# w_in multiplied directly in fp32, and GpSimd's tables, splits and taps given to VectorE

## The chip, the cores and the metric

The kernel runs on one core of one Trainium2 chip. The metric is the device time of one execution in microseconds (us). TensorE is PE in the profile, its weight loads are PEld, VectorE is DVE, ScalarE is ACT, GpSimd is POOL, and SyncE, whose queue issues most DMAs, is SP.

## What is computed

One layer of a hybrid backbone for two groups of 128 tokens of width 1024 (a prompt and a sample, so 256 rows in all), everything in fp32:

```
h = rmsnorm(x) * (1 + sc1) + sh1                 # shifts and scales from c @ w_mod
z = h @ w_in + b_in                              # 1024 -> 5120 columns
z_f, z_a, z_b, z_s, z_g = split(z)               # 512, 512, 512, 512, 3 * 1024
br_f = fft2(z_f).real @ w_four
br_c = conformer_conv(z_a * sigmoid(z_b)) @ w_conv_out      # 31 taps, layer norm, silu
y_s  = s5_bidirectional(z_s)                     # 32 groups, 64 complex states, B, C, D
br_s = glu(gelu(y_s)) @ w_ssm_out
x = x + g1 * ((gate_f*br_f + gate_c*br_c + gate_s*br_s) @ w_out)   # gates: sigmoid(z_g)
x = x + g2 * moe(rmsnorm(x) * (1 + sc2) + sh2)   # top 4 of 32 experts, d_ff 1024
```

The weights of all 32 experts are read, 12 MB for each. The outputs are the two normed results and the final S5 states of the prompt.

## The kernel before, in words

The program has two parts. The **front part** is everything up to the routing; the **expert part** then runs the 32 experts one after the other.

The front part is written as some thirty Python generators ("threads") that yield one instruction at a time. While the program is built, class Sched (L55) plays a list scheduler: for each thread's next instruction it works out when its engine and its operands are ready, from a cost that each helper states (mm, tt, stt, act: L264 to L304), adds 0.2 us per unit of the thread's priority (PRIO), and emits the earliest. That fixes the order on each engine; on the chip every engine then runs its list in that order and waits for semaphores. So a cost that is wrong in the plan shows as a wait on the chip. Every operation of a kind has the line of its helper: L273 is every matmul, L262 every transpose, L291 every tensor_tensor, L287 every scalar_tensor_tensor, L304 every activation.

All large weights come through one ring of slots of 1 MB (class Ring, L169): SP issues the loads in one fixed order, each when a slot comes free. The ring begins with slots 0 to 3 and 6 to 9, of which 6 to 9 are dropped after their first use, so four slots serve most of the front part until the S5 result gives it four more.

The parts of the front that matter here:

- modulate (L517) applies the shift and scale to h, eight blocks k of 128 features. For each block it writes h twice: the rounded half hhi (ACT, in the type fp32r) and the rest hlo (DVE, xT - hhi).
- splitter (L1063) and main_products (L1099) do the big products. Each slab of weights (w_in in twenty slabs of 256 columns, then w_four, w_ssm_out and w_conv_out in two each, w_out in four) is cut in four units of 128x512. split (L769) makes the pair: ACT copies a unit to fp32r, and DVE or POOL subtracts that from the original. Who subtracts is chosen by faster (L765), by whose planned clock is behind. Buffers for four units lie in slots 21 and 22. prod3 (L1089) multiplies hi by hi, hi by lo and lo by hi: three fp32r matmuls of 256 columns in place of one in fp32, so 48 matmuls for a slab.
- the order of slabs (seq) is: eight slabs of w_in for z_s, z_f, z_b, z_a, then for each branch (Fourier, S5, conv) and each half of 512 columns two gate slabs of w_in and the slab of the branch's projection, then w_out. Two gate buffers stand between a pair of gate slabs and its projection, so a later pair waits for the projection before it, which waits for its branch (flags mix0, mix2, mix1).
- tables_in (L803) and tables_out (L825) build the S5 matrices: for each of four quarters j, cprod (L783) runs six tensor_tensors of 128x1024 (four products, two sums). Each table has two threads, one on DVE and one on POOL, that take quarters from one list, each with a temporary of its own. m1_transposes (L810) transposes the first table; its quarters 2 and 3 wait for the flag in0, as their slot holds the first slab of w_in.
- taps_sum(j) (L989) sums the 31 taps of the convolution for 128 channels: for j = 0 to 2, 31 scalar_tensor_tensors of 128x256 on DVE; for j = 3 (NP = 1) ACT multiplies and POOL adds. conv (L1007) norms the sum and ends in mix1.
- s5 (L880) runs its scan of 16 steps on DVE, four tensor_tensors of 128x128 each, in a chain; kernel_table (L835) needs all of tables_out and sends its result through DRAM (the tile Kd) back into SBUF, by DMAs on SP's queue.
- fourier (L1037) and the sum over branches (mac, in evacuate, L1157) use slot 20, which held xT before.

The expert part multiplies each expert's 64 gathered rows by 12 slabs in fp32, with scatter products in fp32r. It is not touched by the change.

Of the kernel before, what the change touches and what calls it, by code (L numbers as in the profile page):

```python
# [205 lines left out]
def build(tc, A, O):  # L206
# [3 lines left out]
    with es:  # L210
# [151 lines left out]
        n = 0  # L362
# [73 lines left out]
        start(6, 7, 8, 9)  # L436
# [27 lines left out]
        hhi = new(4, F32R)[:, :].rearrange("p (k t) -> p k t", k=8)  # L464
        hlo = new(5, F32R)[:, :].rearrange("p (k t) -> p k t", k=8)
# [51 lines left out]
        def modulate():  # L517

            for b in range(4):
# [157 lines left out]
        def s5_inputs():  # L677
# [23 lines left out]
            yield tt(tb[2], Bt[:, 1], bch(fr), e="G")  # L701
            yield tt(tb[1], Bt[:, 1], bch(fi))
            yield tt(tb[3], Bt[:, 0], bch(fi), e="G")
            yield tt(Bb[:, 0], tb[0], tb[1], OP.subtract)
            yield tt(Bb[:, 1], tb[2], tb[3], OP.add, e="G")
# [59 lines left out]
        def faster(n, cv, cg):  # L765

            return "V" if sch.t["V"] + n * cv <= sch.t["G"] + n * cg else "G"
# [13 lines left out]
        Mtmp = [tbuf(SL16[:, 1024:2048]), tbuf(SL[11][:, 1024:2048])]  # L781

        def cprod(o_re, o_im, tmp, P, Q, Qi, j, e):  # L783
# [8 lines left out]
            yield tt(o_re, px(0), qx(Q[0]), e=e)  # L792
            yield tt(tmp, px(1), qx(Q[1]), e=e)
            yield tt(o_re, o_re, tmp, OP.subtract, e=e)
            yield tt(o_im, px(0), qx(Q[1] if Qi is None else Qi), e=e)
            yield tt(tmp, px(1), qx(Q[0]), e=e)
            yield tt(o_im, o_im, tmp, OP.add if Qi is None else OP.subtract, e=e)
# [27 lines left out]
        def tables_out(e, tmp, js):  # L825
            yield from need("E", "columns", "pw1")
            while js:
                j = js.pop(0)
                yield from cprod(M2[j][:, :, 0], M2[j][:, :, 1], tmp, pw2, (Ct[:, 0], Ct[:, 1]), nCi, j, e)
# [50 lines left out]
        def s5():  # L880
# [100 lines left out]
            for o in range(4):  # L981
# [3 lines left out]
                yield from split(g2[:, c], m_[:, c], m_[:, 1024 + 256 * o:1280 + 256 * o], e="V")  # L985
# [3 lines left out]
        def taps_sum(j):  # L989
# [17 lines left out]
        def conv():  # L1007
# [23 lines left out]
            for i in range(2):  # L1031
                c = slice(512 * i, 512 * i + 512)
                yield from split(HA[:, c], m_[:, c], m_[:, 1024 + 512 * i:1536 + 512 * i], e="V")
# [3 lines left out]
        def fourier():  # L1037
            yield from need("zf", "columns", "M10", "M11", "M12", "M13")
            UV = SL[20][:, :].rearrange("p (j b c) -> p j b c", j=4, b=2)
# [11 lines left out]
            for i in range(2):  # L1051
                c = slice(512 * i, 512 * i + 512)
                yield from split(PB[6 + i][:, :], m_[:, c], m_[:, 1024 + 512 * i:1536 + 512 * i], e="V")
# [9 lines left out]
        def splitter():  # L1063
# [5 lines left out]
            for key in seq + [("out", q) for q in range(4)]:  # L1069
                for u in UNITS if key == seq[0] else range(4):  # L1070
# [4 lines left out]
                    elif key[0] == "pr":  # L1075
                        src = sl[:, :].rearrange("p (k c) -> p k c", k=4)[:, :, u * 128:(u + 1) * 128]
                    else:
                        src = sl[:, :].rearrange("p (k c) -> p k c", k=8)[:, 4 * (u % 2):4 * (u % 2) + 4,
                                                                          u // 2 * 128:(u // 2 + 1) * 128]
# [5 lines left out]
                    if u == 3:  # L1085
                        ring.done(key)
                        flags.add("in0")
# [11 lines left out]
        def main_products():  # L1099
            nonlocal mh, ml, xa  # L1100
            yield from need("m0")
            for key in seq:
# [8 lines left out]
                for u in UNITS if key == seq[0] else range(4):  # L1111
                    if key[0] == "in":
                        c, first, last = u // 2, u == 0, u % 2 == 1
                        K, xh, xl = range(4 * (u % 2), 4 * (u % 2) + 4), hhi, hlo
                    else:
                        c, first, last = u % 2, u % 2 == 0, True
# [658 lines left out]
```

## Time and profile before

| | before |
|---|---|
| time, median of 3 runs | 1414.85 us (1414.38 to 1416.57) |
| the profiled execution: time; span | 1418.22 us; 1416.4 us |
| PE, PEld busy | 1243.9 us (88%), 655.7 us (46%) |
| DVE, ACT, POOL busy | 492.4 us (35%), 301.5 us (21%), 216.0 us (15%) |
| mean granted clock of PE | 0.961 |
| moved from HBM | 472.6 MB, 335 GB/s over the span |

The shares are means over two unlike parts. In forty slices of 35.4 us the page shows POOL at 4 to 6 tenths in the first ten slices and at 0 in nearly all later ones; DVE is at 7 to 9 tenths in the same ten and at 1 after them; the DMA engines are at 3 to 9 tenths in the first ten and at 8 or 9 in most later ones.

### The profile page before, as it was taken

Reading aid. Unit: us, or ns where it says so; the run is one execution under the profiler, and the core shown is the slowest. Engines: PE = TensorE matmul, PEld = TensorE weight load, DVE = VectorE, ACT = ScalarE, POOL = GpSimd, SP = SyncE. Lnnn points to the kernel's source line nnn. Section 1 sums busy time; section 2 is a strip of 40 time slices with the busy share of each in tenths; the row PEclk is TensorE's granted clock in tenths of the full one; section 3 lists DMA queues with packets and bytes.
Section 4 is the critical chain, followed back from the end, with each engine's and each line's share of the span. In section 5 each row is a group of like instructions: output and inputs, shape, how many; then the busy total and the mean of one; then the engine's idle time right before and its main releaser. Section 6 shows DMA issues by size and latency. Waiting matters only on the chain. (4 is left out here: it accounts for less than half of the span.)

```text
span 1416.4 us, 19588 instructions
## 1 busy us (share of the span) xinstructions
PE 1243.9 (88%) x7444; PEld 655.7 (46%) x7444; DVE 492.4 (35%) x839; ACT 301.5 (21%) x609; POOL 216.0 (15%) x183
## 2 busy tenths in 40 slices
PE   4596787899999999999989999999999989999994
PEld 3475686789833433334343433333334334343331
DVE  7949898897511111111111111111121111211113
ACT  4454344454311101011100101101011101111011
POOL 4555556565300000000000000000000000000001
PEclk9798899999999999999999999999999999999996
DMA  9563489558799999999998999998999994999990
GB/s 268 193 210 115 144 146 266 188 196 316 290 352 410 416 397 415 416 416 415 417 415 319 407 417 414 415 400 357 416 416 416 416 409 185 413 415 415 414 395 33
DMA packets 124834, 477.08 MB, mean 337 GB/s; under 512 B 11871, under 2 KB 49505, under 8 KB 90864
## 3 DMA queue, kind: packets, MB, share of 16 engines
q1 hardware_dynamic: 121744, 468.25, 85.3%
q0 software_dynamic: 2288, 5.76, 1.2%
q8 instruction: 120, 1.97, 0.6%
q10 hardware_dynamic: 624, 0.63, 0.1%
q14 instruction: 58, 0.48, 0.1%
HBM read 472.61 MB, written 1.61 MB: 335 GB/s over the span
## 5 line engine op out<-in xcount | busy, mean ns | idle before, releaser
L273 PE MATMUL pb<-sl,sl 128*64 128x512 f32 (+4 forms) x5344 | 951.3, 485 | 48.7 <-PEq L1644 13.1
L273 PEld LDWEIGHTS pb<-sl,sl 128*64 128x64 f32 (+2 forms) x5344 | 438.4, 152 | 521.8 <-issue 445.2
L304 ACT ACTIVATE sl<-sl 128x512 fp32r<-128x512 f32 (+4 forms) x211 | 120.8, 588 | 614.2 <-DVE sl L279 496.4
L291 POOL TENSOR_TENSOR sl<-sl,sl 128x512 fp32r<-128x512 f32 (+4 forms) x73 | 121.1, 1667 | 737.5 <-DVE sl L291 607.7
L279 DVE TENSOR_SCALAR sl<-pb 128x512 f32<-128x512 f32 (+1 forms) x35 | 23.7, 676 | 434.7 <-PE pb L273 434.7
L287 DVE SCALAR_TENSOR_TENSOR sl<-pb,wsl,sl 128x512 fp32r<-128x512 f32 x64 | 47.7, 750 | 310.5 <-ACT sl L304 309.3
L291 DVE TENSOR_TENSOR sl<-sl,sl 128x512 fp32r<-128x512 f32 (+3 forms) x107 | 105.6, 1001 | 30.1 <-ACT sl L304 27.7
L304 ACT ACTIVATE sl<-pb 128x512 f32<-128x512 f32 (+6 forms) x125 | 68.5, 585 | 199.2 <-PE pb L273 177.8
L262 PE MATMUL pb<-cst,sl 128*128 128x128 f32 (+2 forms) x354 | 57.4, 296 | 46.0 <-ACT sl L304 15.0
L304 ACT ACTIVATE sl<-pb,wsl 128x512 fp32r<-128x512 f32 x64 | 43.6, 687 | 199.6 <-PE pb L273 196.6
L273 PE MATMUL pb<-sl,PT 128*128 128x512 f32 x256 | 78.0, 428 | 0.5 <-PEq L1644 0.5
L273 PE MATMUL pb<-hb,sl 128*128 128x128 f32 x512 | 68.4, 289 | 7.9 <-DVE hb L291 7.5
L273 PEld LDWEIGHTS pb<-hb,sl 128*128 128x128 f32 x512 | 65.1, 200 | 18.3 <-ACT wsl L304 11.8
L262 PEld LDWEIGHTS pb<-cst,sl 128*128 128x128 f32 (+2 forms) x354 | 43.7, 158 | 63.0 <-issue 26.1
L318 POOL MEMSET sl<- 128x30 f32 (+6 forms) x15 | 2.8, 228 | 374.1 <-PEq L1644 373.8
L287 DVE SCALAR_TENSOR_TENSOR hb<-sl,taps,hb 128x256 f32<-128x256 f32 x90 | 55.5, 664 | 0.6
L273 PEld LDWEIGHTS pb<-sl,PT 128*128 128x128 f32 x256 | 46.2, 201 | 8.0 <-ACT sl L304 1.3
L291 POOL TENSOR_TENSOR sl<-PWT,sl 128x1024 f32<-128x1024 f32 x20 | 43.5, 2190 | 11.1 <-PE pb L273 6.2
L273 PEld LDWEIGHTS pb<-comb,hb 128*128 128x128 f32 x128 | 19.6, 207 | 44.6 <-DVE sl L279 41.9
L291 DVE TENSOR_TENSOR sl<-sl 128x512 f32<-128x512 f32 (+4 forms) x77 | 37.1, 500 | 4.1 <-ACT sl L304 0.5
L273 PE MATMUL pb<-comb,hb 128*128 128x1 f32 x128 | 22.0, 241 | 18.2 <-PEq L1644 16.4
L273 PE MATMUL pb<-ha,selb 128*64 128x512 bf16 (+1 forms) x140 | 21.3, 390 | 16.8 <-PEq L1644 14.4
(176 smaller groups left out, 547.0 us busy)
## 6 DMA issues: line engine op xcount, KB each, us to landing
sl<-w_gate_up SPq DMA_DIRECT2D x256, 1024.0 KB, 14.9
sl<-w_down SPq DMA_DIRECT2D x128, 1024.0 KB, 17.5
sl<-w_mod SPq DMA_DIRECT2D x24, 1024.0 KB, 7.2
sl<-w_in SPq DMA_DIRECT2D x20, 1024.0 KB, 11.1
sl<-w_out SPq DMA_DIRECT2D x4, 1024.0 KB, 6.9
sl<-md POOLq DMA_DIRECT2D x6, 512.0 KB, 6.9
sl<-w_four SPq DMA_DIRECT2D x2, 1024.0 KB
sl<-Kd SPq DMA_DIRECT2D x16, 128.0 KB, 9.2
```

Of the source, the lines that this page charges most:

```text
L262: return sch.op("P", 0.107 * in_.shape[0] / 128, [out], [in_], lambda: te.transpose(out, in_, ident[:in_.shape[0], :in_.shape[0]]))
L273: lambda: te.matmul(out, lhsT, rhs, start=start, stop=stop, skip_group_check=True))
L279: return sch.op(e, c, [o], ap, lambda: ENG[e].tensor_scalar(o, a, s1, None, op0=op0))
L287: lambda: ENG[e].scalar_tensor_tensor(o, a, sc, b, op0=op0, op1=op1))
L291: return sch.op(e, c, [o], [a, b], lambda: ENG[e].tensor_tensor(o, a, b, op=op))
L304: [a] + [x for x in (bias, scale) if hasattr(x, "tensor")], lambda: s.activation(o, a, func, **kw))
L318: return sch.op(e, size(o) * 0.9e-3 + 0.1, [o], [], lambda: ENG[e].memset(o, val))
```

## The change

All products with w_in take the slab as it comes, in fp32, against xT in fp32: 16 matmuls a slab, with no hhi, hlo or splits. Half of the modulations are done by ACT and half by DVE, in place. The pairs stay for the three projections and w_out, and DVE makes all of them. Both S5 tables have one thread, on DVE, and one temporary; all taps are on DVE. The waits for in0 go. Slot 4 joins the ring from the start (hhi's place), slot 5 (hlo's) takes the Fourier buffer and the sum over branches, and slot 20 goes to the ring when the last slab of w_in has been multiplied. The planned cost of an fp32r matmul rises from 4.17e-4 to 4.6e-4 us a column.

```
         def mm(out, lhsT, rhs, start, stop=False):
             if lhsT.dtype != F32:
-                c = max(n, m) * 4.17e-4
+                c = max(n, m) * 4.6e-4
...
-        start(6, 7, 8, 9)
+        start(6, 7, 4, 8, 9)
...
-        hhi = new(4, F32R)[:, :].rearrange("p (k t) -> p k t", k=8)
-        hlo = new(5, F32R)[:, :].rearrange("p (k t) -> p k t", k=8)
...
                     for g in range(2):
-                        yield act(hhi[:, k, 128 * g:128 * g + 128], xT[:, k, g], AF.Identity, bias=modA[:, 0, k, g:g + 1],
-                                  scale=modA[:, 1, k, g:g + 1])
-                        yield ts(xT[:, k, g], xT[:, k, g], modA[:, 1, k, g:g + 1], modA[:, 0, k, g:g + 1])
-                    yield tt(hlo[:, k], flat(xT[:, k]), fv(hhi[:, k]), OP.subtract)
+                        if g:
+                            yield ts(xT[:, k, g], xT[:, k, g], modA[:, 1, k, g:g + 1], modA[:, 0, k, g:g + 1])
+                        else:
+                            yield act(xT[:, k, g], xT[:, k, g], AF.Identity, bias=modA[:, 0, k, g:g + 1], scale=modA[:, 1, k, g:g + 1])
...
-            yield tt(tb[2], Bt[:, 1], bch(fr), e="G")
+            yield tt(tb[2], Bt[:, 1], bch(fr))
...
-        def split(src, hi, lo, e=None):
+        def split(src, hi, lo):
             yield copy(hi, src)
-            yield tt(lo, src, fv(hi), OP.subtract, e=e or faster(size(src), CV, CG))
+            yield tt(lo, src, fv(hi), OP.subtract)
...
-        def tables_in(e, tmp, js):
+        def tables_in(tmp):
             yield from need("Bb", "pw0")
-            while js:
-                j = js.pop(0)
-                yield from cprod(*M1T[j], tmp, pw1, (Bb[:, 0], Bb[:, 1]), None, j, e)
+            for j in range(4):
+                yield from cprod(*M1T[j], tmp, pw1, (Bb[:, 0], Bb[:, 1]), None, j)
...
-                if j == 2:
-                    yield "in0"
...
             for k in range(31):
-                if j >= 4 - NP:
-                    o = 1536 + 256 * (k % 2 if NP == 1 else j % 2)
-                    o = av if k == 0 else SL17[:, o:o + 256].rearrange("p (b t) -> p b t", b=2)
-                    yield act(o, vp[:, j, :, k:k + 128], AF.Identity, scale=taps[:, j, k:k + 1],
-                              **({"bias": vec[:, 40 + j:41 + j]} if k == 0 else {}))
-                    if k:
-                        yield tt(av, av, o, OP.add, e="G")
-                elif k == 0:
+                if k == 0:
                     yield ts(av, vp[:, j, :, 0:128], taps[:, j, 0:1], vec[:, 40 + j:41 + j])
                 else:
                     yield stt(av, vp[:, j, :, k:k + 128], taps[:, j, k:k + 1], av)
...
-            for key in seq + [("out", q) for q in range(4)]:
+            for key in [x for x in seq if x[0] == "pr"] + [("out", q) for q in range(4)]:
...
+                if key[0] == "in":
+                    bk = PB[cnt["bank"] % 2]
+                    yield from bank()
+                    yield lambda: key in ring.ready
+                    w = ring.get(key)[:, :].rearrange("p (k c) -> p k c", k=8)
+                    for n, (k, c) in enumerate((x, c) for x in range(8) for c in range(2)):
+                        if key == seq[0] and c == 0:
+                            yield f"hmod{k}"
+                        yield mm(bk[:, c * 256:(c + 1) * 256], w[:, k, c * 128:(c + 1) * 128], flat(xT[:, k]), n == 0, k == 7)
+                    ring.done(key)
+                    evac.append((key[1], bk))
+                    if key == ("in", seq[-2][1]):
+                        ring.give(20)
+                    continue
```

## Rows read from the trace of the kernel before

**Rows 1.** Busy time by stretch, whole core: start to end, length, then each engine.

```profile
core 0: us, PE busy (x) PEld busy (x) DVE busy (x) ACT busy (x) POOL busy (x), PEclk, DMA share, GB/s
28.00:60.00 32.00, 20.88 (x175) 11.46 (x175) 31.69 (x30) 15.07 (x33) 25.14 (x19) 0.89 0.89 291
60.00:373.00 313.00, 261.44 (x2328) 235.80 (x2329) 255.34 (x368) 149.69 (x306) 169.71 (x133) 0.90 0.64 197
385.00:1400.00 1015.00, 937.93 (x4719) 387.97 (x4718) 164.33 (x278) 120.86 (x239) 3.11 (x6) 0.98 0.96 388
```

**Rows 2.** What PE waited for, 28 to 373 us: total us, times, longest.

```profile
PE pb L273 <- ACT sl L304: 17.2, 6, 11.9
...
PE pb L273 <- DVE sl L291: 10.3, 6, 3.8
PE pb L273 <- POOL sl L291: 7.8, 6, 4.4
...
PE pb L273 <- DMA sl<-Kd: 5.6, 2, 5.3
PE pb L273 <- DVE sl L315: 3.8, 1, 3.8
```

**Rows 3.** DVE in order of time, from several windows: start us, us, instructions.

```profile
43.28 1.21 DVE L291 TENSOR_TENSOR sl<-PWT,sl 128x1024 f32<-128x1024 f32 x1
...
111.59 0.29 DVE L291 TENSOR_TENSOR w<-A8i,sl 128x128 f32<-128x128 f32 x1
...
150.62 1.90 DVE L291 TENSOR_TENSOR w<-A8i,sl 128x128 f32<-128x128 f32 x1
152.44 2.40 DVE L291 TENSOR_TENSOR sl<-sl,sl 128x512 fp32r<-128x512 f32 x1
...
165.49 0.69 DVE L291 TENSOR_TENSOR sl<-sl,sl 128x512 fp32r<-128x512 f32 x1 [0.18 <-ACT sl L304]
...
216.98 2.45 DVE L287 SCALAR_TENSOR_TENSOR hb<-sl,taps,hb 128x256 f32<-128x256 f32 x6
```

**Rows 4.** POOL in order of time, window 151 to 154 us.

```profile
150.40 3.90 POOL L291 TENSOR_TENSOR sl<-PWT,sl 128x1024 f32<-128x1024 f32 x2
```

**Rows 5.** DVE groups by form, 28 to 373 us: busy us, mean ns, idle before.

```profile
L291 DVE TENSOR_TENSOR sl<-sl,sl 128x512 fp32r<-128x512 f32 x74 | 74.9, 1022 | 26.0 <-ACT sl L304 25.5
L287 DVE SCALAR_TENSOR_TENSOR hb<-sl,taps,hb 128x256 f32<-128x256 f32 x90 | 55.5, 664 | 0.6
L291 DVE TENSOR_TENSOR sl<-sl,w 128x128 f32<-128x128 f32 x32 | 23.4, 730 | 0.4
L291 DVE TENSOR_TENSOR sl<-PWT,sl 128x1024 f32<-128x1024 f32 x12 | 19.5, 1647 | 5.4 <-PE pb L273 5.4
L282 DVE TENSOR_SCALAR sl<-sl,modA 128x128 f32<-128x128 f32 x16 | 10.1, 666 | 0.0
L291 DVE TENSOR_TENSOR w<-A8r,sl 128x128 f32<-128x128 f32 x15 | 9.9, 661 | 0.0
L291 DVE TENSOR_TENSOR w<-A8i,sl 128x128 f32<-128x128 f32 x15 | 9.5, 634 | 0.4
```

**Rows 6.** POOL groups by form, 28 to 373 us: busy us, mean ns, idle before.

```profile
L291 POOL TENSOR_TENSOR sl<-sl,sl 128x512 fp32r<-128x512 f32 x50 | 75.8, 1518 | 105.7 <-ACT sl L304 75.1 <-DMA sl<-w_mod 15.1 <-DVE hb L287 7.8
L291 POOL TENSOR_TENSOR sl<-PWT,sl 128x1024 f32<-128x1024 f32 x20 | 43.5, 2190 | 11.1 <-PE pb L273 6.2 <-ACT PWT L304 4.8
L291 POOL TENSOR_TENSOR sl<-sl,sl 128x1024 f32<-128x1024 f32 x11 | 29.6, 2687 | 0.6
L291 POOL TENSOR_TENSOR hb<-hb,sl 128x256 f32<-128x256 f32 x30 | 24.8, 827 | 29.5 <-ACT sl L304 28.3
```

**Rows 7.** PE in order of time: a run of fp32r products; the GLU's sixteen fp32 matmuls.

```profile
172.63 6.63 PE L273 MATMUL pb<-sl,sl 128*128 128x256 f32 x54
...
238.42 6.97 PE L273 MATMUL pb<-sl,sl 128*128 128x256 f32 x32
```

**Rows 8.** PE groups by form, 60 to 373 us: the products of 256 columns.

```profile
L273 PE MATMUL pb<-sl,sl 128*128 128x256 f32 x1472 | 204.0, 299 | 24.1 <-DVE sl L291 10.3 <-POOL sl L291 7.8 <-ACT sl L304 5.0
```

More of the change, by code (lines that the diff above doesn't have):

```diff
@@ L700, in s5_inputs @@
             yield tt(tb[0], Bt[:, 0], bch(fr))
-            yield tt(tb[2], Bt[:, 1], bch(fr), e="G")
+            yield tt(tb[2], Bt[:, 1], bch(fr))
             yield tt(tb[1], Bt[:, 1], bch(fi))
-            yield tt(tb[3], Bt[:, 0], bch(fi), e="G")
+            yield tt(tb[3], Bt[:, 0], bch(fi))
             yield tt(Bb[:, 0], tb[0], tb[1], OP.subtract)
-            yield tt(Bb[:, 1], tb[2], tb[3], OP.add, e="G")
+            yield tt(Bb[:, 1], tb[2], tb[3], OP.add)
             flags.add("Bb")
@@ L791, in qx @@
                 return a[:, gs, None, :].to_broadcast([128, 8, 8, 16])
[L792 to L797, printed above, removed]
+            yield tt(o_re, px(0), qx(Q[0]))
+            yield tt(tmp, px(1), qx(Q[1]))
+            yield tt(o_re, o_re, tmp, OP.subtract)
+            yield tt(o_im, px(0), qx(Q[1] if Qi is None else Qi))
+            yield tt(tmp, px(1), qx(Q[0]))
+            yield tt(o_im, o_im, tmp, OP.add if Qi is None else OP.subtract)
         def need(*f):
@@ L823, in m1_transposes, with tables_out @@
                 flags.add(f"M1{j}")
-        def tables_out(e, tmp, js):
+        def tables_out(tmp):
             yield from need("E", "columns", "pw1")
-            while js:
-                j = js.pop(0)
-                yield from cprod(M2[j][:, :, 0], M2[j][:, :, 1], tmp, pw2, (Ct[:, 0], Ct[:, 1]), nCi, j, e)
+            for j in range(4):
+                yield from cprod(M2[j][:, :, 0], M2[j][:, :, 1], tmp, pw2, (Ct[:, 0], Ct[:, 1]), nCi, j)
                 flags.add(f"M2{j}")
@@ L984, in s5 @@
                 yield tt(g2[:, c], g1[:, c], g2[:, c])
-                yield from split(g2[:, c], m_[:, c], m_[:, 1024 + 256 * o:1280 + 256 * o], e="V")
+                yield from split(g2[:, c], m_[:, c], m_[:, 1024 + 256 * o:1280 + 256 * o])
             mixhi[2], mixlo[2] = j4(m_[:, 0:1024]), j4(m_[:, 1024:2048])
@@ L1032, in conv @@
                 c = slice(512 * i, 512 * i + 512)
-                yield from split(HA[:, c], m_[:, c], m_[:, 1024 + 512 * i:1536 + 512 * i], e="V")
+                yield from split(HA[:, c], m_[:, c], m_[:, 1024 + 512 * i:1536 + 512 * i])
             mixhi[1], mixlo[1] = j4(m_[:, 0:1024]), j4(m_[:, 1024:2048])
@@ L1052, in fourier @@
                 c = slice(512 * i, 512 * i + 512)
-                yield from split(PB[6 + i][:, :], m_[:, c], m_[:, 1024 + 512 * i:1536 + 512 * i], e="V")
+                yield from split(PB[6 + i][:, :], m_[:, c], m_[:, 1024 + 512 * i:1536 + 512 * i])
             mixhi[0], mixlo[0] = j4(m_[:, 0:1024]), j4(m_[:, 1024:2048])
@@ L1068, in splitter @@
             n = 0
-            for key in seq + [("out", q) for q in range(4)]:
-                for u in UNITS if key == seq[0] else range(4):
+            for key in [x for x in seq if x[0] == "pr"] + [("out", q) for q in range(4)]:
+                for u in range(4):
                     yield lambda: key in ring.ready and cnt["used"] >= n - NW + 1
@@ L1074, in splitter @@
                         src = sl[:, u * 512:(u + 1) * 512].rearrange("p (k c) -> p k c", k=2)
-                    elif key[0] == "pr":
+                    else:
                         src = sl[:, :].rearrange("p (k c) -> p k c", k=4)[:, :, u * 128:(u + 1) * 128]
-                    else:
-                        src = sl[:, :].rearrange("p (k c) -> p k c", k=8)[:, 4 * (u % 2):4 * (u % 2) + 4,
-                                                                          u // 2 * 128:(u // 2 + 1) * 128]
                     b = slice(512 * (n % NW), 512 * (n % NW) + 512)
@@ L1086, in splitter @@
                         ring.done(key)
-                        flags.add("in0")
         def prod3(out, whi, wlo, xhi, xlo, first, last):
@@ L1110, in main_products @@
                     yield f"mix{i}"
[L1111 to L1116, printed above, removed]
-                        K, xh, xl = range(4), mixhi[i], mixlo[i]
-                    if first:
+                if key[0] == "in":
[12 more added lines that the diff above has]
+                    continue
+                for u in range(4):
+                    c = u % 2
+                    if c == 0:
                         bk = PB[cnt["bank"] % 2]
@@ L1122, in main_products @@
                     hi, lo = spl.pop((key, u))
-                    for n, k in enumerate(K):
-                        if key == seq[0]:
-                            yield f"hmod{k}"
-                        yield from prod3(bk[:, c * 256:(c + 1) * 256], hi[:, n], lo[:, n], xh[:, k], xl[:, k], first and n == 0,
-                                         last and n == 3)
+                    for k in range(4):
+                        yield from prod3(bk[:, c * 256:(c + 1) * 256], hi[:, k], lo[:, k], mixhi[i][:, k], mixlo[i][:, k],
+                                         c == 0 and k == 0, k == 3)
                     cnt["used"] += 1
-                    if key[0] == "in" and u == 3:
-                        evac.append((key[1], bk))
-                    elif key[0] == "pr" and c == 1:
+                    if c == 1:
                         evac.append((key, u // 2, bk))
-                if key == ("in", seq[-2][1]):
-                    new(4)
-                    new(5)
-                    ring.give(4, 5)
             for q in range(4):
@@ L1171, in evacuate @@
                         yield tt(gat[q], bk[:, :], gat[q])
-                        yield tt(mac, mac, gat[q], OP.add, e="V" if i == ORDER[2] else faster(512, 1.1e-3, 2e-3))
+                        yield tt(mac, mac, gat[q], OP.add)
                         if i == ORDER[2]:
@@ L1175, in evacuate @@
                             if h and q:
-                                ring.give(20)
+                                ring.give(5)
                 elif isinstance(job[0], tuple):
@@ L1366, in build @@
                          ("m1", m1_transposes((0, 1), (PB[3], PB[5]))), ("m1", m1_transposes((2, 3), (PB[6], PB[7]))),
-                         ("in", tables_in("V", Mtmp[0], js[0])), ("in", tables_in("G", Mtmp[1], js[0])),
+                         ("in", tables_in(Mtmp)),
                          ("columns", late_columns()),
-                         ("out", tables_out("V", Mtmp[0], js[1])), ("out", tables_out("G", Mtmp[1], js[1])),
+                         ("out", tables_out(Mtmp)),
                          ("kernel", kernel_table()), ("conv", conv()), ("fourier", fourier()), ("main", main_products()),
@@ L1747 @@
 KS = 4
-UNITS = 0, 2, 1, 3
 MA = 0
@@ L1751 @@
 ORDER = (0, 2, 1)
-NP = 1
-CV = 0.0016
-CG = 0.0016
 COLS_AT = 'R0'
```

11 lines of the change are left out of this document (4 added, 7 removed).

## The prediction, made before the changed kernel was run

> **What bounds the kernel now.** I read the busy time by stretch first [rows 1]. Two stretches carry the time. From 385 to 1400 us the experts run: PE is busy 938 of 1015 us, the DMA engines 0.96 of it, POOL hardly at all. Nothing of the change runs there, so its length is taken as fixed, and what counts is when it starts. From 60 to 373 us, in the front part, PE is busy 261.4 of 313 us at a mean clock of 0.90, DVE 255.3 (82%), POOL 169.7. In the 32 us before that, DVE is busy 31.7. So DVE has almost no slack until the last projections, while PE has 51.6 us of idle time.
>
> The waits of PE come next [rows 2]: it stands still for ACT (17.2 us), for DVE's subtractions (10.3) and for POOL's (7.8), which are the pairs and the copies behind them, and for little else: 5.6 us for Kd and 3.8 us for the convolution's sums.
>
> Third, DVE in order of time [rows 3]. One step of the S5 scan takes 0.29 us at 111.59 and 1.90 at 150.62; a pair's subtraction takes 0.69 us at 165.49 and 2.40 at 152.44. What differs is POOL: at 150.40 it begins two products of 128x1024, 3.90 us together [rows 4], and DVE's instructions end with POOL's. DVE hardly works beside POOL; it waits it out. The groups give the amount [rows 5], busy time less count times the short duration of rows 3: pairs 74.9 - 74 x 0.69 = 23.8; taps 55.5 - 90 x 0.41 = 18.6 (six in 2.45 us); scan 23.4 - 32 x 0.29 = 14.1, 9.9 - 15 x 0.29 = 5.6 and 9.5 - 4.4 = 5.2; table products 19.5 - 12 x 1.21 = 5.0. Together 72 us of DVE's 287 between 28 and 373 us are waiting for POOL. And POOL is no quicker at the same work: 1.5 us for a pair against 0.69, 2.19 for a table product against 1.21 [rows 3, 6].
>
> **The change, part by part.** The sum is made for the profiled execution, span 1416.4 us, reported at 1418.2, which is 3.4 us over the median of 1414.85; a shift of the experts' start is taken over to the median unchanged.
>
> *PE.* The pairs' matmuls take 6.63 / 54 = 0.123 us each, three to a product, 0.368. The GLU has the same form as the new products (128x128 weights from a slab, 256 columns, fp32); its sixteen matmuls take 6.97 us, 0.436 each, in two records [rows 7]. For 20 slabs x 16 products w_in goes from 117.9 to 139.4 us: **21.5 us more on PE**.
>
> *DVE.* Of its 74 subtractions and POOL's 50, 124 in all, 80 belong to w_in and go; DVE makes the other 44, so 30 fewer, -20.7 us. Eight modulations at 0.67 and the eight hlo subtractions (priced as a tap, 0.41) go: -8.6 us. It gains POOL's 30 table instructions (20 products and, without one addition to x, 10 sums) [rows 6] at 1.21: +36.3; the fourth tap sum, 31 x 0.41 = 12.7; three small products of Bb at 0.69, near 20 us, +2. With the 72 us of stretch gone: 287 - 72 - 20.7 - 8.6 + 36.3 + 12.7 = 235 us, where 287 were. DVE goes from the pace to some 78% of the stretch.
>
> *ACT* loses 80 copies and 31 taps and takes no more modulations than before (8 where 16 were); it was busy 149.7 of 313 us and stays behind the others. It costs nothing.
>
> *POOL's and SP's queues.* POOL's small DMAs (biases, md, the second load of x) stand behind less work; nobody is later for it. On SP the order is as before, with slot 4 as a fifth slot from the start, so each slab of w_in may be asked for one slab earlier. The slots 4, 5 and 20 change places at the end: one comes free at the start, 20 with the last slab of w_in, 5 with the last sum. The number that the first expert finds is the same, so the experts should start with the same lead of their loads; if they don't, the third rival prices it. M1's quarters 2 and 3 lose their wait for in0, which is no longer due as the slab lies elsewhere.
>
> *The start.* Between 28 and 60 us DVE is full [rows 1], and sixteen modulations take 0.67 us each in the mean [rows 5]. With POOL silent and eight fewer, but twelve of POOL's first-table instructions waiting behind them, I take the first slab's product 6 us earlier, at 54 instead of 60; bounds are 0 and 10 us.
>
> *The new sum.* What else PE does from 60 to 373 is 261.4 - 204.0 = 57.4 us if all 204 us of the group of row 8 are its own [rows 1, 8]; but 1440 pair products at 0.123 and the GLU make only 183.8, so up to 77.6 us. I take 64, nearer to the first, as the group's surplus is mostly half clock and waiting in its own runs. After: 139.4 (w_in) + 480 x 0.123 = 59.0 (the projections' pairs) + 7.0 (GLU) + 64 = 269.4 us. Waiting: DVE's and ACT's part goes, Kd and the convolution's sums stay, 9.4 us. So PE ends the projections at 54 + 269 + 9 = 333 us where it was 373: the experts start **40 us earlier**, and PE has become what sets the pace. 1414.85 - 40 = 1375.
>
> What is late next: the S5 result (mix2) and the convolution (mix1), each in front of a projection. After mix2 PE still has six slabs of w_in and eight of pairs, 6 x 16 x 0.436 + 8 x 48 x 0.123 = 89 us, so mix2 may be no later than some 240 us; before, it came after the GLU that stands at 238 [rows 7]. It would have to lose its stretched scan and tables only, not to gain.
>
> A rule that speaks against this: the Trainium skill, Perfetto Trace Analysis, Optimizing Scalar/DVE Operations, says that where DVE is saturated, giving work to ScalarE or even GpSimd may make sense; by that, bringing GpSimd's work back to a DVE that is 82% busy goes the wrong way, to the second rival's time. The same section limits itself: the two share a read port, so moving work between them might not help. Rows 3 and 4 side with the limit.
>
> **The rivals.** *One: the idle time stays.* If PE's idle time comes from the chains of S5 and the convolution rather than from the pairs, the work shifts but the 51.6 us remain: 54 + 269 + 52 = 375, 2 us later, 1417. For it: the largest single wait is one of 11.9 us for ACT; against it: the waits named in rows 2 are mostly for pairs and copies, and DVE's load falls by 50 us in both chains.
>
> *Two, slower: DVE's long durations are its own.* If 0.69 and 0.29 us are the exceptions, the new work comes at the means of rows 5: tables 30 x 1.647 = 49.4, taps 31 x 0.664 = 20.6, less pairs 30 x 1.022 = 30.7 and modulations 5.3: 34 us more on an engine already full, 1449. It decides as soon as DVE's pair still takes 1.0 us in the mean with POOL idle. Against it stand the paired times of rows 3 and 4.
>
> *Three: the experts don't start their loads earlier.* If their first slabs come late, the 40 us turn into waiting at the first experts: 1415. The DMA engines were 0.64 busy before 373 us, so there is room [rows 1]; it would take a slot that frees late.
>
> **How the numbers follow.** The forecast and its smaller forms have 0.89, the first rival 0.05, the third 0.02, the second 0.04. Moved alone, the unknowns of the sum give: rest of PE 57 or 78 us, -47 or -26; waiting 0 or half the old idle time (26), -49 or -23; start 50 or 60, -44 or -34. Two bad or two good ones together give about -11 and -57, so 1358 to 1404. That holds 0.8; the rivals and a gain under 11 us lie outside. About 0.2% (2.8 us) is what a measurement can tell from no change: faster 0.89, same 0.07 (rivals one and three), slower 0.04.
>
> **What would show it.** Right: POOL without work from 28 to 330 us; DVE's pairs at 0.69 us and scan steps at 0.29 throughout; PE over 90% busy between first slab and projections, w_in at 0.43 us a product in two records; the first expert's matmul near 345 us; the expert stretch still about 1015 us. Wrong: DVE still over 90% busy or its means still long (rival two); gaps of PE over 30 us in all, before the projections (rival one); a wait of PE for w_gate_up at the first experts, or a longer expert stretch (rival three); a product of w_in over 0.5 us, which would add 20 us.

## The result, and the profile after

| | before | after |
|---|---|---|
| time, median | 1414.62 us (1413.87 to 1416.57, 4 runs) | 1370.67 us (1369.51 to 1373.99, 4 runs) |
| ratio to before | | 0.9691, 95% interval 0.967 to 0.9712 |
| the profiled execution: time; span | 1418.22 us; 1416.4 us | 1371.8 us; 1370.0 us |
| first product of w_in, first expert's product | 66.79, 385.13 us | 45.35, 340.83 us |

The kernel became 44 us faster; 40 were forecast. The page of the changed kernel, its span, busy times and three lines of its forty slices:

```profile
span 1370.0 us, 18609 instructions
PE 1247.5 (91%) x7146; PEld 645.4 (47%) x7146; DVE 418.2 (31%) x858; ACT 241.6 (18%) x490; POOL 42.1 (3%) x69
...
PE   5999789999999999999999999999999989999994
...
POOL 1000101201000000000000000000000000000001
PEclk9999989999999999999999999999999999999997
```

POOL has next to nothing left to do in the front, PE is at 7 to 9 tenths from the second slice on, and its clock is at 9 tenths or more in nearly all of the front. POOL was to be without work from 28 to 330 us; it is not quite, as the 24.5 us in the second row below are memsets, small DMAs and four tensor_tensors (one at 241 us, three from 306 on), but none of it is a table, a pair or a tap. Busy time by stretch, to be held against [rows 1] (whole core; length, then each engine, the clock, the DMA share):

```profile
core 0: us, PE busy (x) PEld busy (x) DVE busy (x) ACT busy (x) POOL busy (x), PEclk, DMA share, GB/s
28.00:60.00 32.00, 31.24 (x254) 19.08 (x255) 27.70 (x43) 17.41 (x40) 0.87 (x8) 1.00 1.04 345
45.00:328.00 283.00, 266.71 (x2017) 225.17 (x2010) 199.43 (x386) 91.82 (x192) 24.52 (x32) 0.98 0.73 228
340.00:1354.00 1014.00, 939.61 (x4723) 390.09 (x4723) 165.24 (x284) 121.00 (x240) 3.12 (x6) 0.99 0.96 388
```

From the first slab of w_in to the end of the projections PE is busy 94% of 283 us; the expert stretch is as long as it was, 1014 us. What PE still waits for, 28 to 373 us (total, times, longest), answers to [rows 2]; the second row lies in the expert part, at 361.6 us:

```profile
PE pb L273 <- DMA sl<-Kd: 13.8, 1, 13.8
PE pb L273 <- DVE hb L291: 2.3, 1, 2.3
PE pb L273 <- DVE sl L315: 1.1, 2, 0.6
PE pb L273 <- ACT sl L304: 1.1, 2, 0.7
```

The waits for pairs and copies are gone; one for Kd is left, and it is longer than the 5.6 us of before. The groups of DVE, 28 to 330 us (busy us, mean ns, idle before), answer to [rows 5]:

```profile
L287 DVE SCALAR_TENSOR_TENSOR hb<-sl,taps,hb 128x256 f32<-128x256 f32 x120 | 49.8, 477 | 0.3
L291 DVE TENSOR_TENSOR sl<-PWT,sl 128x1024 f32<-128x1024 f32 x32 | 37.8, 1219 | 6.8 <-PE pb L273 6.7
L291 DVE TENSOR_TENSOR sl<-sl,sl 128x512 fp32r<-128x512 f32 x44 | 31.0, 729 | 29.2 <-ACT sl L304 28.7
...
L291 DVE TENSOR_TENSOR sl<-sl,w 128x128 f32<-128x128 f32 x32 | 9.2, 288 | 0.5
```

All 120 taps take less together than 90 did before (49.8 and 55.5 us), 32 table products 37.8 us where 12 took 19.5, and an instruction of the scan (the last row) 288 ns in the mean where it took 730.

The start shows POOL's hold on DVE best. Before, DVE and POOL in order of time while the scales of the first block are made (start, us, instruction):

```profile
38.55 2.91 POOL L291 TENSOR_TENSOR sl<-PWT,sl 128x1024 f32<-128x1024 f32 x1
...
41.42 1.92 POOL L291 TENSOR_TENSOR sl<-PWT,sl 128x1024 f32<-128x1024 f32 x1
...
36.29 3.38 DVE L291 TENSOR_TENSOR sl<-PWT,sl 128x1024 f32<-128x1024 f32 x1
39.59 0.18 DVE L315 TENSOR_REDUCE pm<-pb 128x8 f32<-128x32 f32 x1
39.81 1.67 DVE L291 TENSOR_TENSOR modA<-pm,vec 128x8 f32<-128x8 f32 x1
41.51 1.84 DVE L287 SCALAR_TENSOR_TENSOR modA<-modA,vec 128x4 f32<-128x4 f32 x1
...
51.74 4.72 DVE L282 TENSOR_SCALAR sl<-sl,modA 128x128 f32<-128x128 f32 x2
```

and DVE after:

```profile
36.82 0.19 DVE L315 TENSOR_REDUCE pm<-pb 128x8 f32<-128x32 f32 x1 [2.77 <-PE pb L262]
37.05 0.17 DVE L291 TENSOR_TENSOR modA<-pm,vec 128x8 f32<-128x8 f32 x1
37.25 0.16 DVE L287 SCALAR_TENSOR_TENSOR modA<-modA,vec 128x4 f32<-128x4 f32 x1
37.45 0.60 DVE L282 TENSOR_SCALAR sl<-sl,modA 128x128 f32<-128x128 f32 x2
```

An instruction on eight elements a partition took 1.67 us, ten times its 0.17, and ended at 41.48, just behind POOL's first product (41.46); the next ended at 43.35, just behind the second (43.34). The reduction, which reads PSUM and not SBUF, took 0.18 beside the same POOL instruction. PE in order of time, the first product of w_in and the first expert's before, and then after:

```profile
66.79 3.12 PE L273 MATMUL pb<-sl,sl 128*128 128x256 f32 x13
...
385.13 1.94 PE L273 MATMUL pb<-sl,sl 128*64 128x512 f32 x8
...
45.35 0.70 PE L273 MATMUL pb<-sl,sl 128*128 128x256 f32 x2
...
144.58 6.74 PE L273 MATMUL pb<-sl,sl 128*128 128x256 f32 x30
...
177.65 4.63 PE L273 MATMUL pb<-sl,sl 128*32 128x128 f32 x66 [13.79 <-DMA sl<-Kd]
...
340.83 1.94 PE L273 MATMUL pb<-sl,sl 128*64 128x512 f32 x8
```

So the gain in the trace is 385.13 - 340.83 = 44.3 us before the experts: 66.79 - 45.35 = 21.4 at the start, and 22.9 between the first slab and the first expert. The span fell by 46.4 us; the other 2.1 lie behind the first expert's product (1031.3 us to the end before, 1029.2 after).

### The profile page after: what moved, and what is told of

It reads as the page before. It is cut to its first block, busy times and chain, and to the rows that moved or that the text cites. A ratio compares the mean times of both kernels' runs of the same rounds, so it can differ in the third digit from the quotient of the medians.

```text
span 1370.0 us, 18609 instructions
## 1 busy us (share of the span) xinstructions
PE 1247.5 (91%) x7146; PEld 645.4 (47%) x7146; DVE 418.2 (31%) x858; ACT 241.6 (18%) x490; POOL 42.1 (3%) x69
## 5 line engine op out<-in xcount | busy, mean ns | idle before, releaser
L273 PE MATMUL pb<-sl,sl 128*64 128x512 f32 (+5 forms) x5024 | 959.2, 507 | 32.1 <-PEq L1623 14.5
L273 PEld LDWEIGHTS pb<-sl,sl 128*64 128x64 f32 (+2 forms) x5024 | 431.9, 147 | 515.8 <-issue 450.5
L304 ACT ACTIVATE sl<-sl 128x512 f32<-128x512 f32 (+5 forms) x131 | 72.6, 564 | 559.2 <-DVE sl L279 496.0
L279 DVE TENSOR_SCALAR sl<-pb 128x512 f32<-128x512 f32 (+1 forms) x35 | 23.6, 676 | 434.5 <-PE pb L273 434.5
L262 PE MATMUL pb<-cst,sl 128*128 128x128 f32 (+2 forms) x354 | 53.8, 282 | 28.1 <-DMA sl<-ssm_b_re 8.4
L291 DVE TENSOR_TENSOR sl<-sl,sl 128x512 fp32r<-128x512 f32 (+3 forms) x80 | 65.1, 833 | 32.9 <-ACT sl L304 30.9
L262 PEld LDWEIGHTS pb<-cst,sl 128*128 128x128 f32 (+2 forms) x354 | 40.5, 149 | 47.0 <-issue 14.3
L287 DVE SCALAR_TENSOR_TENSOR hb<-sl,taps,hb 128x256 f32<-128x256 f32 x120 | 49.8, 477 | 0.3
L291 DVE TENSOR_TENSOR sl<-PWT,sl 128x1024 f32<-128x1024 f32 x32 | 37.8, 1219 | 6.8 <-PE pb L273 6.7
L273 PE MATMUL pb<-comb,hb 128*128 128x1 f32 x128 | 21.6, 237 | 17.7 <-PEq L1623 15.9
L273 PE MATMUL pb<-ha,selb 128*64 128x512 bf16 (+1 forms) x140 | 21.4, 390 | 17.1 <-PEq L1623 14.0
L291 POOL TENSOR_TENSOR sl<-sl,sl 128x512 f32<-128x512 f32 (+3 forms) x11 | 16.4, 1503 | 671.3 <-DVE sl L291 656.4
L273 PE MATMUL pb<-sl,cs 128*32 128x256 f32 (+1 forms) x320 | 30.4, 439 | 0.7 <-PEq L1623 0.7
```

The costliest lines, as they stand in the source:

```text
L262: return sch.op("P", 0.107 * in_.shape[0] / 128, [out], [in_], lambda: te.transpose(out, in_, ident[:in_.shape[0], :in_.shape[0]]))
L279: return sch.op(e, c, [o], ap, lambda: ENG[e].tensor_scalar(o, a, s1, None, op0=op0))
L287: lambda: ENG[e].scalar_tensor_tensor(o, a, sc, b, op0=op0, op1=op1))
L291: return sch.op(e, c, [o], [a, b], lambda: ENG[e].tensor_tensor(o, a, b, op=op))
L304: [a] + [x for x in (bias, scale) if hasattr(x, "tensor")], lambda: s.activation(o, a, func, **kw))
```

## The experiments

The theory: DVE waited POOL out, and the pairs of w_in loaded DVE; with both gone PE sets the pace. The rivals give the gain to one half of the change, to the planner's corrected cost, to the fifth slot, or make the long durations DVE's own.

**pairs_dve**: the kernel before with POOL's share alone moved.

```
-            yield tt(lo, src, fv(hi), OP.subtract, e=e or faster(size(src), CV, CG))
+            yield tt(lo, src, fv(hi), OP.subtract, e="V")
...
-                         ("in", tables_in("V", Mtmp[0], js[0])), ("in", tables_in("G", Mtmp[1], js[0])),
+                         ("in", tables_in("V", Mtmp[0], js[0])),
...
-NP = 1
+NP = 0
```

> The kernel before, w_in still in pairs, but everything that POOL did in the front (splits, tables, taps) on DVE. Theory (the stretch of DVE is POOL's doing, and both halves of the change are needed): DVE loses its 72 us of stretch and gets 50 subtractions at 0.69, 30 table instructions at 1.21, 31 taps at 0.41 and 2 us of small products, 85 us: 287 - 72 + 85 = 300 us of work where 287 were busy. Scan steps at 0.29 us and pairs at 0.69 throughout, but DVE stays the pace of the front: 1405 to 1428 us, ratio to before 0.993 to 1.01. Rival A (moving POOL's share is the whole gain): 1368 to 1385. Rival B (the long durations are DVE's own): pairs still near 1.0 us in the mean, over 1440.

**fp32_pool**: the changed kernel with POOL's share given back.

```
-            yield tt(lo, src, fv(hi), OP.subtract)
+            yield tt(lo, src, fv(hi), OP.subtract, e=e or faster(size(src), 0.0016, 0.0016))
...
-                         ("in", tables_in(Mtmp)),
+                         ("in", tables_in("V", Mtmp[0], js[0])), ("in", tables_in("G", Mtmp[1], js[0])),
...
+                if j == 3:
...
+                    yield act(o, vp[:, j, :, k:k + 128], AF.Identity, scale=taps[:, j, k:k + 1],
...
+                    if k:
+                        yield tt(av, av, o, OP.add, e="G")
```

> The changed kernel (w_in in fp32) with POOL's share of before given back: both tables on two threads, the splits that are left to the engine whose planned clock is behind, the fourth tap sum on ACT and POOL. Theory: the pairs of w_in gone is the larger part of the gain, POOL's contention the smaller: DVE's scan steps and taps come out stretched again wherever POOL works (means over 0.40 and over 0.55 us), the S5 chain ends 10 to 20 us later than in the changed kernel and PE waits that much longer for it: 1380 to 1392 us. Rival A (contention costs nothing once the pairs of w_in are gone): 1368 to 1374. Rival C (the gain is POOL's silence alone): 1405 or more.

Measured, the four corners (medians; ratio to before with its interval):

| | w_in in pairs | w_in in fp32 |
|---|---|---|
| POOL's share on POOL | before | 1424.72 us; 1.006 (1.004 to 1.0079) |
| POOL's share on DVE | 1422.22 us; 1.0049 (1.0027 to 1.0071) | 1370.67 us; 0.9691 (0.967 to 0.9712) |

Each half alone makes the kernel a little slower, by 0.5% and 0.6%; only both together win. For fp32_pool that is far outside the theory's 1380 to 1392: giving POOL its share back costs 54 us there, not 10 to 20. Read alone it is in the range of rival C (the gain is POOL's silence alone), but pairs_dve has that silence and no gain; and rival A of pairs_dve, the same claim, is out by 37 us.

Busy time from the first product of w_in to the first expert's, for the kernel before, pairs_dve, fp32_pool and the changed kernel, in this order:

```profile
67.00:385.00 318.00, 269.75 (x2457) 243.52 (x2456) 258.60 (x388) 149.75 (x308) 172.15 (x135) 0.91 0.66 207
45.00:390.00 345.00, 267.77 (x2494) 239.72 (x2490) 262.88 (x516) 143.60 (x285) 27.80 (x35) 0.87 0.64 198
59.00:397.00 338.00, 290.44 (x2161) 243.02 (x2159) 205.76 (x342) 108.51 (x231) 119.64 (x103) 0.92 0.63 195
45.00:341.00 296.00, 278.85 (x2176) 236.19 (x2170) 209.95 (x422) 95.59 (x203) 27.70 (x35) 0.98 0.74 232
```

pairs_dve has the whole early start of the changed kernel, with its pairs and all sixteen modulations on the same engines as before, and then gives it back: PE is idle 77 us where it was idle 48. fp32_pool starts 7.5 us earlier than the kernel before, PE has 21 us more work, which is the price that was forecast for the fp32 products, and it is idle 48 us as before. Only in the changed kernel does the idle time fall, to 17 us.

PE's granted clock is the number before the last two: 1.0 is its upper level (2.4 GHz), and it is below that in a mean because it falls to 0.5 (1.2 GHz) for a while; in the changed kernel it did so once, from 167.6 to 181.3 us, while PE stood before Kd from 163.9 on. At the lower level a matmul took twice as long (before, 0.49 us at 130.51, where the same took 0.24 at 116.68). PE was busy 34, 29, 30 and 4 us of the four stretches at that level, so by an estimate, half of that, the lower clock cost 17, 14, 15 and 2 us. It goes with some 15 us of the whole gain, but it is not what made the halves lose.

In pairs_dve the scan's instructions took 288 ns and the pairs 705, so the stretch was indeed POOL's. Its first product of w_in, and what PE waited for (28 to 385 us):

```profile
45.40 3.26 PE L273 MATMUL pb<-sl,sl 128*128 128x256 f32 x25
...
PE pb L273 <- DMA sl<-Kd: 27.4, 1, 27.4
PE pb L273 <- ACT sl L304: 17.1, 8, 13.5
PE pb L273 <- DVE sl L279: 13.5, 2, 13.3
PE pb L273 <- DVE sl L315: 9.7, 2, 7.4
```

Hardly for pairs (5.1 us), but for the S5 table (the rows of Kd and of L279, which follows the table on DVE) and the convolution (its sums, L315, and 13.5 us before its pairs): 47 of the 124 subtractions, 32 us of them, stand on DVE between the second table's products, which run from 104.7 to 193.1 us (81.3 to 133.9 in the changed kernel). The expected time was right, its reason only in part: DVE was to have 300 us of work between 28 and 373, and was busy 265. So DVE need not be busy all the time to be the limit: it was busy 239.5 of 313 us from 60 to 373, and the chain that goes through it was late.

In fp32_pool the first product of w_in came at 59.3 us, and the scan at 107 to 148 us instead of 87 to 112. POOL, DVE, ACT and PE in order of time, 112 to 140 us:

```profile
120.20 3.90 POOL L291 TENSOR_TENSOR sl<-PWT,sl 128x1024 f32<-128x1024 f32 x2
...
122.24 2.01 DVE L291 TENSOR_TENSOR w<-A8r,sl 128x128 f32<-128x128 f32 x1
...
126.83 0.85 ACT L304 ACTIVATE sl<-sl 64x128 f32<-64x128 f32 x2 [4.70 <-DVE sl L291]
...
136.41 2.08 PE L273 MATMUL pb<-cst,sl 128*128 128x256 f32 x4 [11.21 <-ACT sl L304]
```

A stretched scan does not stop at DVE: ACT copies each state (the 64x128 rows) and waits for every step, the evacuations behind those copies wait too, and PE waits 11.2 us for one of them. The 11.9 us for ACT in [rows 2] were the same: ACT waited 9.4 us for the scan's states in front of the copy that PE needed.

**fp32_in** and **fp32_tables** split POOL's share up: only its part of the first table and of Bb, and both tables, each in the changed kernel. fp32_tables is fp32_pool with `e="V"` in split and in the sums over branches (mac) and no tap sum on POOL; fp32_in also drops this thread:

```
-                         ("out", tables_out("V", Mtmp[0], js[1])), ("out", tables_out("G", Mtmp[1], js[1])),
+                         ("out", tables_out("V", Mtmp[0], js[1])),
```

> The changed kernel with POOL's part of the first S5 table and of Bb given back alone. Theory: the cost of the first table on POOL is the later start, because DVE's small modulation instructions stand beside it: first w_in product at 57 to 61 us, scan steps at 0.29 us afterwards; of the 34 us that both tables cost, 12 to 18 here: 1383 to 1391 us. Rival (the second table, beside the scan, carries it): 1371 to 1378.

> The changed kernel with POOL's part of the S5 tables and of Bb given back alone (splits and taps stay on DVE). Theory: the tables are the part that costs most, since the first one stands beside the modulations in front of the first slab and the second beside the scan: first w_in product at 57 to 61 us as with the whole share given back (59.3), not at 45.3, scan steps over 0.40 in the mean: 1385 to 1412 us. Rival (splits and taps on POOL cost it): 1370 to 1380.

Measured: fp32_in 1386.89 us, 0.9797 (0.9769 to 0.9825); fp32_tables 1404.97 us, 0.9903 (0.9883 to 0.9922). Both as expected, so the price is now split: 1386.9 - 1370.7 = 16 us for the first table, 18 more for the second, and 1424.7 - 1405.0 = 20 more for splits, taps and the sums over branches, taken in this order. In fp32_in the first product came at 59.4 us and the scan's instructions took 288 ns again, so 14 of its 16 us are the later start (45.35 in the changed kernel), with modulations of 1073 ns in the mean instead of 344.

**beside_tt** and **beside_set** put useless work on POOL beside the scan: a small product that reads a state of the scan, and then ten additions, or ten memsets in their place.

```
+        def beside():
+            yield fill(scr[:, :], 0.0)
+            yield "c3"
+            yield tt(scr[:, 0:128], SL[13][:, 384:512], SL[13][:, 384:512], e="G")
+            for _ in range(10):
+                yield tt(scr[:, :], scr[:, :], scr[:, :], OP.add, e="G")
```

> The changed kernel with eleven additions put on POOL from the fourth step of the S5 scan on (one of 128x128, ten of 128x512 on a buffer that nobody needs then), results unused. Theory (a POOL tensor_tensor stops DVE's until it ends): ten POOL instructions of near 1.65 us each stand in front of a DVE instruction of the scan, which then ends with them (1.6 to 1.9 us instead of 0.29), some 13 us later in all; the scan ends near 124 us instead of 111, and as the S5 chain is what PE waits for, PE's wait for Kd grows by most of it: 1377 to 1386 us. Rival (the long durations are DVE's own, or come from something else that went): scan steps at 0.29, 1368 to 1374.

> The same with ten memsets of 128x512 on POOL in place of the additions, which read nothing. Theory (what DVE waits for is POOL's reading of operands): the scan steps stay at 0.29 us and the time at 1368 to 1374. Rival (any instruction of POOL on the same memory does it): as with the additions, scan steps that end with POOL's memsets.

Measured: beside_tt 1377.51 us, 0.9722 (0.9705 to 0.9738); beside_set 1369.5 us, 0.9665 (0.9649 to 0.9682). POOL and DVE with the additions:

```profile
91.14 9.26 POOL L291 TENSOR_TENSOR hb<-hb 128x512 f32<-128x512 f32 x8
...
93.49 0.28 DVE L291 TENSOR_TENSOR w<-A8r,sl 128x128 f32<-128x128 f32 x1
93.70 2.24 DVE L291 TENSOR_TENSOR sl<-sl,w 128x128 f32<-128x128 f32 x2
95.97 1.08 DVE L291 TENSOR_TENSOR w<-A8i,sl 128x128 f32<-128x128 f32 x1
```

and with the memsets:

```profile
91.88 5.77 POOL L318 MEMSET hb<- 128x512 f32 x10
...
92.53 0.29 DVE L291 TENSOR_TENSOR w<-A8i,sl 128x128 f32<-128x128 f32 x1
...
92.95 0.61 DVE L291 TENSOR_TENSOR sl<-sl,w 128x128 f32<-128x128 f32 x2
```

Beside POOL's additions three of four of the scan's instructions take 1.1 us, about one addition each; beside its memsets all take 0.29. So POOL's writing alone does not hold DVE up, and its additions, which read SBUF too, do; no run parts the reading from the kind of instruction. This kernel pays it in full: the scan ended 6 us later (117.6 and 111.7) and the kernel 7. The size was half of what was expected, as these additions took 1.1 us and not 1.65, and every fourth instruction slipped through. Nor did it come where it was expected: PE's wait for Kd stayed (14.1 us), and a wait of 6.5 us for ACT was new, up to 105.17 us, by the same way through ACT's copies of the states that fp32_pool shows. The Trainium skill, SBUF — State Buffer, Who interferes with whom, states a rule for this: a DVE instruction with two SBUF inputs contends with a GpSimd instruction that reads SBUF, not with one that only writes it. These two runs agree with it.

**plan417** and **slot4late** undo the two small parts.

```
-                c = max(n, m) * 4.6e-4
+                c = max(n, m) * 4.17e-4
```

```
-        start(6, 7, 4, 8, 9)
+        start(6, 7, 8, 9)
...
-                        ring.give(20)
+                        ring.give(4, 20)
```

> The changed kernel with the planned cost of an fp32r matmul as before (4.17e-4 us a column). Theory: a detail of the order, 1368 to 1376 us. Rival D (the corrected plan is a part of the gain): 1380 or more.

> The changed kernel with slot 4 given to the ring with slot 20, at the last slab of w_in, so that four slots serve the front as before. Theory: loads of the front have room (DMA share 0.72 of the stretch), so a slot less costs little: 1370 to 1378 us. Rival E (the fifth slot is a part of the gain, PE then waits for slabs): 1382 or more, with waits of PE for w_in or w_mod in the trace.

Measured: 1368.63 us, 0.9666 (0.9638 to 0.9694), and 1372.53 us, 0.9698 (0.9676 to 0.9721). Neither can be told from the changed kernel; the planner's cost and the slot are no part of the gain that could be measured.

**out_first** and **kd_plan** go after the wait for Kd that is left.

```
-PRIO = {... 'out': 2.0, ...}
+PRIO = {... 'out': -12.0, ...}
```

```
-                self.t[e[0]] = end = self.fit("H", end, 0.45)
+                self.t[e[0]] = end = self.fit("H", end, 0.9 if any(r[0] == "Kd" for r in ins + outs) else 0.45)
```

> The changed kernel with the second S5 table ahead of the scan on DVE (its thread's priority from 2.0 to -12). Theory (what is left of PE's waiting is the chain table, Kd, M3): the table ends some 20 us earlier, the way of Kd through DRAM runs beside the scan, and PE's wait of 13.8 us for Kd goes or falls under 4: 1354 to 1364 us. Rival (the scan or the conv then ends that much later and PE waits for it instead): 1368 to 1380.

> The changed kernel with one planned cost raised: each of the 32 DMAs of Kd occupies the planner's issue queue for 0.9 us and not 0.45. Theory (what is left of PE's waiting is a plan that thinks M3 is home some 14 us too early, so that its matmuls stand in PE's order in front of products that were ready; that is also why the table ahead of the scan did not help): some 18 more fp32 products and some 30 of the pairs come ahead of them, PE's wait for Kd falls from 13.8 to under 3 us with M3 landing when it did: 1356 to 1364 us. Rival (those products only move, because the S5 result is then what the next projection waits for): 1367 to 1375.

Measured: out_first 1375.93 us, 0.9703 (0.9687 to 0.972); kd_plan 1366.88 us, 0.9644 (0.9626 to 0.9663). In out_first the table ended 26 us earlier and the S5 result came at 169 us instead of 183, but PE's wait for Kd did not move. Its longest wait in out_first:

```profile
PE pb L273 <- DMA sl<-Kd: 13.7, 1, 13.7
```

PE runs its list in order: M3, the S5 matrix that is read back from Kd, was home at 163.1 us instead of 177.7, but the matmuls that need it had moved forward in the list as well, and PE stood before them from 149.4 instead of 163.9. The expectation that Kd's way would be covered was wrong; the time is in the range of its rival. In kd_plan the list changed instead:

```profile
177.20 0.64 PE L273 MATMUL pb<-sl,sl 128*32 128x128 f32 x4 [5.87 <-DMA sl<-Kd]
179.10 3.63 PE L273 MATMUL pb<-sl,sl 128*32 128x128 f32 x60 [1.26 <-DMA sl<-Kd]
```

M3 is home at the same time as in the changed kernel (177.20 and 177.65), but PE came to it 7.5 us later with work done (171.3 and 163.9). The wait halved, from 13.8 to 7.1 us, and the time fell by 3.8 us. The mechanism held; the size missed 1356 to 1364. The list moved by 50 matmul records where some 66 were expected; whether a still larger planned cost would move more of them was not run. kd_plan is the fastest version found; its interval lies below that of the changed kernel, though the two were timed in different sets of runs against the same kernel before.

**pairs_out** and **pairs_out_kd** ask whether pairs_dve was only badly ordered: the two edits above, first one and then both, on pairs_dve.

> w_in in pairs, POOL's share on DVE (as in pairs_dve, 1422.2), and the second S5 table ahead of the scan and the splits on DVE (its thread's priority from 2.0 to -12). In pairs_dve that table stood between the splits from 104 to 193 us. Theory (the pairs of w_in and the S5 chain need DVE at the same time, so whoever goes first delays the other): the table ends near 145 us and mix2 earlier, but PE then waits for pairs while the table runs: 1398 to 1418 us. Rival F (only the order was bad; with the pairs' cheaper products PE would end as early as in the changed kernel): 1385 or less.

> The same, with 0.9 us planned for each of Kd's 32 DMAs as in kd_plan. Theory: PE's wait for Kd (27.4 us in pairs_dve) shrinks where other products are ready, which here need pairs from DVE: 5 to 15 us under pairs_out, still over 1385. Rival F: 1375 or less, at or under the changed kernel.

Measured: 1423.94 us, 1.006 (1.0038 to 1.0083), a little above the range given, and 1412.78 us, 0.9986 (0.9975 to 0.9996). With the table first its last product ended at 131.6 us instead of 193.1, and PE waited elsewhere. Its two longest waits in pairs_out, 60 to 385 us:

```profile
PE pb L262 <- DVE sl L291: 21.8, 1, 21.8
PE pb L273 <- DVE sl L291: 21.0, 3, 20.1
```

20.1 us of the second row are one wait at 113.4 us for a pair, while DVE made the table. In pairs_out_kd the time fell as far as expected, but not as expected: PE's wait for Kd went from 11.3 to 10.6 us only, the 21.8 us of the first row to 5.9, and its wait for the convolution's sums rose from 2.1 to 13.4. So pairs of w_in and the S5 chain do want DVE at the same time, and these two orders only choose who waits. That no order of this version comes near 1370 was not shown; two were tried.

## Why the prediction was right, and where it was not

**PE's new work: right.** A product of w_in was to take 0.436 us in two records; 30 records took 6.74 us, 0.449 a product, so 143.7 us for w_in instead of 139.4. The whole group of 1152 records (w_in, the projections' pairs, the GLU) took 211.0 us from 28 to 333, where the sum had 205.4.

**What PE does besides: taken too high.** 64 us was taken between 57.4 and 77.6. PE was busy 266.7 us; less the group's 211.0 that is 56, at the lower end. With it goes a granted clock of 0.98 where it was 0.90 in [rows 1].

**The waiting that stays: mis-sized.** 9.4 us was forecast as the waits for Kd and the convolution's sums of before; 283 - 266.7 = 16.3 us was measured, 13.8 of it Kd. The step treated a wait as a constant. It is not one: it depends on how much work stands ahead of M3's matmuls in PE's list, as kd_plan shows. That the way through DRAM was covered before by products that were held up themselves fits this, but no run shows it.

**The wait for ACT: misread.** The 17.2 us for ACT were put down to the pairs and the copies behind them, and with them to the part that goes. 11.9 of them were the scan, which held up ACT. They did go, but with POOL's share: fp32_pool, without a pair of w_in, still has 11.2 us of them, and pairs_dve, with all the pairs, has no such wait in its scan.

**The start: taken far too small.** It said 6 us earlier, at 54 instead of 60, with bounds of 0 and 10. The first product stood at 66.79, not at the edge of the stretch that was read, and it came at 45.35: 21.4 us. The row that priced it was the modulations' mean of 0.67 us; the small instructions in front of them, with 0.17 us of work and 1.67 us of waiting, were not looked at. With POOL's part of the first table and of Bb alone given back the start came 14 us later (fp32_in). In pairs_dve, where only POOL's share was moved, the first product came at 45.40: moving that share is enough for all 21 us, while dropping the pairs and half of the modulations gives 7.5 by itself (fp32_pool, 59.3).

The errors were of opposite signs: 45 + 283 = 328 for the end of the projections, where 54 + 269 + 9 = 333 had been summed, and 44 us where 40 were. That the two lie so near each other is in part luck: against the sum, the start came 9 us earlier, PE had 3 us less to do, and it waited 7 us longer.

**DVE: right in kind, its relief taken too small.** 235 us were forecast, 216 were busy from 28 to 333 us (27.7 to 60 us and 188.5 behind). The stretch was more than the 72 us of the groups that were summed: the modulations, the subtractions of 128x256 and the small instructions of the start fell by 17.7 us together, where 8.6 had been summed, and other small groups had it too. A tap came as forecast, 49.8 / 120 = 0.415 us of busy time.

**What the prediction did not see: the interaction.** It summed DVE's load part by part and priced no half by itself; the expectation of 1380 to 1392 us for fp32_pool shows that each part was thought to give its share. Alone, each gave a loss. Without POOL but with pairs, DVE had 124 subtractions and all tables, and the S5 chain came late; with fp32 but with POOL, PE paid for its dearer products and the chain was still stretched.

**The rivals.** One (the idle time stays) did not happen here, with 16 us left of 51.6, but it is what pairs_dve did: 74 us of idle PE from 60 to 373. Two (the durations are DVE's own) is excluded by beside_tt against beside_set. Three (the experts' loads come late) is excluded by the 1029.2 us from the first expert's product to the end, where 1031.3 were.

The Trainium skill, Perfetto Trace Analysis, Optimizing Scalar/DVE Operations, says that a saturated DVE may hand work to GpSimd, and that this might not help as the two share a read port. The runs side with the limit where DVE had room: from a DVE busy 71% (216 of 305 us), giving the work to GpSimd cost 54 us. They do not speak against the first half: with the pairs, on a DVE that was 82% busy, taking GpSimd's work back was no gain but 0.5% slower.

## What to carry to other kernels

A DVE instruction that takes several times its usual duration may be waiting, although the profile counts it as busy: compare its shortest and its mean duration, and look at what POOL does at that time. Before splitting a change into parts, ask which queue both parts load: relief in one place can be worth nothing while the chain through the other is as late as before, and two parts that lose alone may win together. In an engine that runs a planned list in order, look at what stands ahead of a wait in the list: here a truer planned cost halved the wait for Kd, and an earlier start of its chain did not shorten it.

## What was not expected of the hardware

- The waiting follows POOL's instruction and not the size of the waiting one: 128x4 elements took 1.84 us beside POOL's products, 128x128 took 2.36 (4.72 for two), and a reduction out of PSUM beside the first of them 0.18.
- POOL seems to wait for DVE as well: its product at 38.55 us, which began beside DVE's product of 3.38 us (1.21 alone), took 2.91 us, and the next, beside an instruction of 128x4, took 1.92. So the means of [rows 6] hold waiting too. No run was made for this.
- Instructions with one tensor from SBUF were held too: the modulations (TENSOR_SCALAR, 128x128) took 1073 ns in the mean in fp32_in and 344 in the changed kernel.
- POOL's ten memsets of 128x512, 5.8 us together, delayed no scan step.
